# A two-layer float32 trunk: the last output group's weights in the rooms of two activation pairs, their norms put last, and the first chunks queued ahead of two weights

## The chip, the cores and the metric

One core of one Trainium2 chip runs the whole program. TensorE (PE) does the matmuls and transposes, VectorE (DVE) and ScalarE (ACT) the element work, GpSimd (POOL) some small work and the stores of hidden tiles and of the residual, SyncE (SP) issues all loads. The metric is the device time of one execution in microseconds (us). The kernel before took 2356.33 us, the median of three runs (2354.39 to 2356.82).

## The reference

Two layers over a sequence of 1024 tokens of width 1024, all float32. Layer 0 mixes tokens with a state-space model and a gated projection, layer 1 with a short gated convolution. Each is followed by a SwiGLU feed-forward part (FFN) and a gated per-layer embedding (PLE):

```python
for i in range(DEPTH):
    hn = rmsnorm(h, norm_mix_g[i])
    mix = s5_mixer(hn, ...) if i % 2 == 0 else shortconv_mixer(hn, ...)
    h = h + mix
    h = h + swiglu_ffn(rmsnorm(h, norm_ffn_g[i]), ffn_w_in[i], ffn_w_out[i])   # hidden width 2816
    gate = jax.nn.sigmoid(rmsnorm(h, norm_ple_g[i]) @ ple_w_gate[i])
    h = h + gate * (p[i] @ ple_w_up[i])
return rmsnorm(h, final_norm_g)
```

## The kernel before

A float32 matmul is done as three matmuls of reduced-precision parts (`mm3`, L121 to L124): each operand is split into a high part, rounded by an ACT cast (L87), and a low part, the rest, by a DVE subtract (L88); the products are high by high, high by low, low by high. Tokens stand in 8 tiles of 128, taken in the order 0, 4, 1, 5, 2, 6, 3, 7; tiles q and q+4 are pair q.

The FFN's hidden tensor (22 blocks of 128 columns) is written to DRAM (`hid`, by GpSimd, L322) and read back by `out_phase` (L326), which multiplies it with the output weights. It takes the 22 weights in three groups, of 8, 8 and 6. For a group it goes over the 8 tiles; a tile loads its hidden chunks (`ch`, four blocks each, L346; 512 KB for a full one), in the first group also the residual `h` (L348), runs 24 matmuls per full chunk (four weights, two halves of the columns, three products) into two PSUM banks (PE's shape in the rows: `psmm<-ulow,ch`, `psmm<-uhigh,ch` or `psmm<-w,ch`, by where the weight stands), and adds them to `h` (L360). The first group's weights are fetched ahead (L332). A weight of the next group marked early is fetched after a tile, one per tile (`soon`); the others when the group has ended (`late`). The same function serves `conv_out`, the output projection of the convolution, with 8 weights in two groups of 4.

Weights and activations share rooms in SBUF. `ulow[:, q]` is the room of pair q's activations or of two weights (`room_low(q, s)`); `uhigh` holds six weights (`room_high`); four more stand in `w8` tiles (`room_new`). In the FFN the groups stand in: the eight low rooms; high 0 to 5 and new 0, 1; new 2, 3 and high 0 to 3. The last four are late, since the second group's weights stand in high 0 to 3 until it ends.

Every load passes through one of four staging slots, `r0` to `r3` (`raw_tile`), taken in rotation in program order: weights before their split (`raw`, L100), chunks, and the normed tiles `xn` of `norm_pair` (L173). A tile gets its slot when the last reader of the tile four places earlier has ended, and SP issues its loads in order: what waits at its head holds all behind it.

After the last group each tile is handed on (`last_post`, L366). For the FFN that is `norm_tile`: the tile is normed, transposed and split into `ulow[:, q]`, from which the PLE part starts, tiles again in the order above. For `conv_out` it is `norm_pair` for the next FFN's first matrix, which uses a seven-product (Strassen-like) block scheme: pair q is normed when tile q+1 is handed on, pair 3 after tile 7. Of a pair, 4 blocks of transposes (L181) go to PE, 2 norms (`xn`, L173), 4 sums (L221 to L232) and 7 subtracts (L88) to DVE. The weights of the next matrix (`weights_set`, L268) need 4 sums (L275 to L283) and 7 subtracts on DVE.

The order of instructions on each engine comes from a scheduler that runs when the program is built. An engine executes its list in order.

Of the kernel before, what the change touches and what calls it, by code (L numbers as in the profile page):

```python
# [23 lines left out]
def trunk(  # L24
# [12 lines left out]
    KT = D // P  # L37
# [26 lines left out]
    HT = T // 2  # L64
# [17 lines left out]
    def psum(pool=None):  # L82
        pool = pool or mm
        return pool.tile([P, 512], F32, name="ps" + pool.name, tag="ps")
# [7 lines left out]
    def raw_tile(i=None, shape=(P, D), dt=F32, name="raw"):  # L92
        if i is None:
            slots.append(slots.pop(0))
        tag = slots[-1] if i is None else f"r{i}"
        return (uhp if tag == "r3" else rawp).tile(list(shape), dt, name=name, tag=tag)

    def load_raw(src, pattern, **kw):
        raw = raw_tile()
        nc.sync.dma_start(out=raw.rearrange(pattern, **kw), in_=src)  # L100
        return raw


    def slot_low(q, s):
        v = ulow[:, q, s * 2 * D:(s + 1) * 2 * D].rearrange("p (l n) -> p l n", l=2)
        return v[:, 0], v[:, 1]

    def slot_high(i):
        v = uhigh.rearrange("p c k l j -> p (c k l j)")[:, i * 2 * D:(i + 1) * 2 * D].rearrange("p (l n) -> p l n", l=2)
        return v[:, 0], v[:, 1]  # L110
# [5 lines left out]
    def unit_of(slot, raw):  # L116
        hi, lo = slot
        split(hi, lo, raw)
        return hi, lo

    def mm3(ps, ahi, alo, bhi, blo, start, stop, more=False):  # L121
        PE.matmul(ps, ahi, bhi, start=start, stop=False, skip_group_check=more)  # L122
        PE.matmul(ps, ahi, blo, start=False, stop=False, skip_group_check=more)  # L123
        PE.matmul(ps, alo, bhi, start=False, stop=stop, skip_group_check=more)  # L124
# [4 lines left out]
    def first():  # L129
        return tc.high_priority(offset=100)  # L130

    def square(t, cs):

        if "ms" not in squares:
            squares["ms"] = tiny.tile([P, T, 4], F32, name="ms", tag="ms")
        got = squares.setdefault(t, [])
        junk = t2_tile("junk", BF16, D)
        ms = squares["ms"][:, t, len(got):len(got) + 1]
        A.activation(junk[:, cs], h[t][:, cs], AF.Square, scale=1.0 / math.sqrt(D), accum_out=ms)  # L139
        got.append(ms)  # L140
# [13 lines left out]
    def load_gain(g_row):  # L154
        gb = tiny.tile([P, D], F32, name="gb", tag="gb")
        nc.gpsimd.dma_start(out=gb, in_=g_row.partition_broadcast(P))
        return gb
# [49 lines left out]
    def norm_pair(q, gb):  # L207
        t0, t1 = q, q + HT
        halves = 2 if q == HT - 1 else 1
        x0, x1 = normed(t0, gb, halves), normed(t1, gb, halves)  # L210

        def put(c, src):
            split(moving_part(c, 0, q), moving_part(c, 1, q), by_kt(src))

        p11, p12, p22 = transposed(x0, 0), transposed(x1, 0), transposed(x1, 1)
        p21 = transposed(x0, 1, mm)
        put(0, p11)
        b12 = t2_tile("b12")
        A.copy(b12, p12)
        T1 = t2_tile("T1")  # L220
        V.tensor_tensor(T1, b12, p11, ALU.subtract)  # L221
        T2 = t2_tile("T2")
        V.tensor_tensor(T2, p22, T1, ALU.subtract)
        put(1, T2)
        put(2, T1)
        put(3, p21)
        T3 = t2_tile("T3")
        V.tensor_tensor(T3, p22, b12, ALU.subtract)
        put(4, T3)
        put(5, p22)  # L230
        T4 = t2_tile("T4")
        V.tensor_tensor(T4, p21, T2, ALU.subtract)  # L232
        put(6, T4)

    def spill(t):
        nc.gpsimd.dma_start(out=hdram[t], in_=h[t])
# [89 lines left out]
    def out_phase(wout, groups, last_post, following=()):  # L326


        def fetch(ht, room):
            return unit_of(room(), load_raw(wout[ht], "p n -> p n"))  # L330

        units = {ht: fetch(ht, room) for ht, room, _ in groups[0]}  # L332
        for gi, group in enumerate(groups):
            last = gi == len(groups) - 1
            todo = [(early, lambda ht=ht, room=room: units.__setitem__(ht, fetch(ht, room)))
                    for ht, room, early in ([] if last else groups[gi + 1])]
            todo = todo or list(following)
            soon, late = [f for early, f in todo if early], [f for early, f in todo if not early]
            for t in ORDER:
                parts = {}  # L340
                for ht, *_ in group:
                    if ht // 4 not in parts:
                        parts[ht // 4] = ch = raw_tile(shape=(P, 4, 2, P), dt=F32R, name="ch")
                        of = [x[0] % 4 for x in group if x[0] // 4 == ht // 4]
                        ks = slice(min(of), max(of) + 1)
                        nc.sync.dma_start(out=ch[:, ks].bitcast(F32), in_=hid[ht // 4][t, :, ks])  # L346
                if gi == 0:
                    nc.sync.dma_start(out=h[t], in_=hdram[t])  # L348
                ps = [psum() for _ in range(2)]
                for j in parts:  # L350
                    mine = [x[0] for x in group if x[0] // 4 == j]
                    for nb in range(2):
                        cs = slice(nb * 512, (nb + 1) * 512)
                        for ht in mine:
                            ch = parts[j][:, ht % 4]
                            bhi, blo = (w[:, cs] for w in units[ht])
                            mm3(ps[nb], ch[:, 0], ch[:, 1], bhi, blo, ht == group[0][0], ht == group[-1][0])
                        if mine[-1] == group[-1][0]:
                            with first():
                                V.tensor_tensor(h[t][:, cs], ps[nb], h[t][:, cs], ALU.add)  # L360
                                if last:
                                    square(t, cs)
                if soon:
                    soon.pop(0)()
                if last:
                    last_post(t)  # L366
            for f in soon + late:
                f()

    def room_low(q, s):  # L370
        return lambda: slot_low(q, s)

    def room_high(i):
        return lambda: slot_high(i)

    def room_new(i):
        return lambda: slot_new(i)
# [18 lines left out]
    def ffn_out(l, post, following):  # L396
        rooms = [(room_low(q, s), False) for s in range(2) for q in range(HT)]
        rooms += [(room_high(i), True) for i in range(6)] + [(room_new(i), True) for i in range(4)]
        rooms += [(room_high(i), False) for i in range(4)]
        hts = [(ht, *room) for ht, room in enumerate(rooms)]  # L400
        cuts = [0, 8, 16, NHT]
        out_phase(ffn_w_out[l].rearrange("(ht p) n -> ht p n", p=P), [hts[a:b] for a, b in zip(cuts, cuts[1:])], post,
                  following)

    def ple_units(l, nb, rooms):

        wg = ple_w_gate[l].rearrange("(kt p) n -> p kt n", p=P)
        units = {}

        def fetch(u):  # L410
            raw = load_raw(wg[:, 2 * u:2 * u + 2, nb * 512:(nb + 1) * 512], "p (kt n) -> p kt n", kt=2)
            units[u] = [a.rearrange("p (kt n) -> p kt n", kt=2) for a in unit_of(rooms[u](), raw)]

        return units, [lambda u=u: fetch(u) for u in range(KT // 2)]
# [595 lines left out]
    def posted(gain, pairs):  # L1010

        gb = load_gain(gain)

        def pair(q):
            norm_pair(q, gb)
            spill(q)
            spill(q + HT)

        def post(t):
            if not pairs:  # L1020
                return norm_tile(t, gb)
            if 0 < t < HT:
                pair(t - 1)
            if t == T - 1:
                pair(HT - 1)
        return post
# [17 lines left out]
        h_tiles()  # L1044

    def ffn_ple(l, last):
        units, makers = ple_units(l, 0, [room_high(i) for i in (4, 5, 0, 1)])
        ffn_out(l, posted(norm_ple_g[l], False), [(i < 2, f) for i, f in enumerate(makers)])
        if last:
            gb = load_gain(final_norm_g)  # L1050
            ple(l, units, lambda t: final_tile(t, gb))
        else:
            ple(l, units, posted(norm_mix_g[l + 1], True))
# [12 lines left out]
    inner("f1", lambda: ffn_in(1), (11, 3, 7, 3))  # L1066
    outer("f1", 4)
    ffn_ple(1, True)
    release()

# [29 lines left out]
```

## Time and profile before

| | |
|---|---|
| median of 3 runs | 2356.33 us |
| profiled execution, time / span | 2359.43 us / 2357.5 us |
| PE busy, mean granted clock | 2247.0 us (95% of the span), 0.981 |
| DVE, ACT, POOL busy | 1331.9, 765.5, 163.1 us |

PE is busy nearly all the time, so what matters is where it stands still, what it waits for there, and where its granted clock is low. Layer 0's FFN output starts at 848 us and its last group at 1046 us of the span, layer 1's at 1998 and 2194 us; the convolution's output projection ends at 1557 us.

### The profile page before, as it was taken

How to read it: one execution, taken by the hardware profiler on the slowest of the kernel's cores; microseconds unless marked ns; L12 is line 12 of the kernel's file. 1: busy time of each engine (PE TensorE's matmuls, PEld its weight loads, DVE VectorE, ACT ScalarE, POOL GpSimd, SP SyncE). 2: the span in 40 equal slices, each digit the busy share in tenths (PEclk: the TensorE clock that was granted, in tenths of full speed). 3: DMA queues.
4: the chain of work that ended last, by engine and by line, in shares of the span. 5: the costliest groups of instructions: out<-in, count | busy, mean ns of one | idle time of the engine just before them, and what ended most of it. 6: DMA issues, size and time to landing. Idle time of an engine off the chain costs nothing.

```text
span 2357.5 us, 27090 instructions
## 1 busy us (share of the span) xinstructions
PE 2247.0 (95%) x10253; PEld 1835.7 (78%) x10253; DVE 1331.9 (56%) x2246; ACT 765.5 (32%) x1449; POOL 163.1 (7%) x268
## 2 busy tenths in 40 slices
PE   6888999899999999999979999989999999999998
PEld 4776887788888878878858888768888888788787
DVE  7785326866666642125488776487666666121454
ACT  6554223433333320013343332153333333000232
POOL 2110001000000000000000000010000001000000
PEclk8999999999999999999989999999999999999999
DMA  7555202333333364333232225434333335543333
GB/s 246 141 135 148 69 1 89 105 112 112 111 114 110 107 241 149 118 127 114 70 129 81 90 92 179 159 125 125 108 108 107 111 113 172 212 139 107 108 109 110
DMA packets 212978, 288.87 MB, mean 123 GB/s; under 512 B 21360, under 2 KB 152432, under 8 KB 212848
## 3 DMA queue, kind: packets, MB, share of 16 engines
q1 hardware_dynamic: 191520, 212.63, 29.0%
q0 software_dynamic: 20928, 74.47, 10.2%
q8 instruction: 80, 1.31, 0.2%
q14 instruction: 50, 0.41, 0.1%
q10 hardware_dynamic: 400, 0.04, 0.0%
HBM read 190.93 MB, written 79.69 MB: 115 GB/s over the span
## 4 chain that ended last, share of the span: by engine, by line
PE 85%; DMA 6%; DVE 5%; ACT 1%; SPq 1%; issue 1%; POOL 0%; DVEq 0%; POOLq 0%; ACTq 0%
PE psmm L122 27%; PE psmm L124 27%; PE psmm L123 27%; DMA ch<-hid 2%; PE pstr L181 1%; DMA raw<-in_ffn_w_out_dram 1%; DMA tw<-tmp 1%; DVE W L575 1%; DVE gv L925 1%; DMA h<-hd 1%; DVE tmp L575 1%; DVE ulow L88 1%; DVE uhigh L88 1%; PE pstr L874 0%; DVE raw L575 0%
## 5 line engine op out<-in xcount | busy, mean ns | idle before, releaser
L122 PE MATMUL psmm<-ulow,ws 128*128 128x512 f32 x896 | 351.1, 393 | 1.6 <-ACT s L301 1.6
L123 PE MATMUL psmm<-ulow,ws 128*128 128x512 f32 x896 | 350.6, 391 | 0.0
L124 PE MATMUL psmm<-ulow,ws 128*128 128x512 f32 x896 | 350.4, 391 | 0.0
L124 PE MATMUL psmm<-uhigh,ws 128*128 128x512 f32 x672 | 265.3, 395 | 0.0
L122 PE MATMUL psmm<-uhigh,ws 128*128 128x512 f32 x672 | 265.1, 394 | 0.0
L123 PE MATMUL psmm<-uhigh,ws 128*128 128x512 f32 x672 | 264.9, 394 | 0.0
L360 DVE TENSOR_TENSOR h<-psmm,h 128x512 f32<-128x512 f32 x128 | 88.0, 690 | 276.6 <-PE psmm L124 276.6
L88 DVE TENSOR_TENSOR ws<-raw,ws 128x512 fp32r<-128x512 f32 x224 | 153.6, 688 | 117.8 <-ACT ws L87 117.4
L87 ACT CAST ws<-raw 128x512 fp32r<-128x512 f32 x224 | 137.5, 619 | 213.0 <-PE psmm L124 211.2
L122 PEld LDWEIGHTS psmm<-ulow,ws 128*128 128x128 f32 x896 | 169.4, 189 | 39.5 <-ACT s L301 2.9
L123 PEld LDWEIGHTS psmm<-ulow,ws 128*128 128x128 f32 x896 | 169.4, 189 | 36.2
L124 PEld LDWEIGHTS psmm<-ulow,ws 128*128 128x128 f32 x896 | 169.2, 189 | 36.2
L87 ACT CAST ws<-st 128x512 fp32r<-128x512 f32 x168 | 104.0, 620 | 204.4 <-PE psmm L124 189.5
L123 PEld LDWEIGHTS psmm<-uhigh,ws 128*128 128x128 f32 x672 | 126.1, 188 | 30.3
L124 PEld LDWEIGHTS psmm<-uhigh,ws 128*128 128x128 f32 x672 | 126.1, 188 | 30.3
L122 PEld LDWEIGHTS psmm<-uhigh,ws 128*128 128x128 f32 x672 | 126.1, 188 | 29.1
L323 POOL DMA_DIRECT2D hid<-hs x104 | 78.2, 755 | 903.4 <-DVE hs L88 895.4
L122 PE MATMUL psmm<-ulow,ch 128*128 128x512 f32 x320 | 128.4, 401 | 10.8 <-DMA ch<-hid 10.8
L139 ACT ACTIVATE junk<-h 128x512 bf16<-128x512 f32 (+1 forms) x113 | 64.0, 567 | 204.0 <-DVE h L360 104.0
L87 ACT CAST uhigh<-raw 128x1024 fp32r<-128x1024 f32 x36 | 37.2, 1049 | 278.9 <-PE psmm L124 136.7
L123 PE MATMUL psmm<-ulow,ch 128*128 128x512 f32 x320 | 127.6, 399 | 0.0
L124 PE MATMUL psmm<-ulow,ch 128*128 128x512 f32 x320 | 127.5, 398 | 0.0
(240 smaller groups left out, 4238.5 us busy)
## 6 DMA issues: line engine op xcount, KB each, us to landing
hid<-hs POOLq DMA_DIRECT2D x104, 512.0 KB, 4.3
ch<-hid SPq DMA_DIRECT2D x96, 512.0 KB, 3.7
raw<-in_ffn_w_in_dram SPq DMA_DIRECT2D x88, 512.0 KB, 4.4
raw<-in_ffn_w_out_dram SPq DMA_DIRECT2D x44, 512.0 KB, 3.6
hd<-h POOLq DMA_DIRECT2D x24, 512.0 KB, 3.0
h<-hd SPq DMA_DIRECT2D x24, 512.0 KB, 8.7
raw<-in_conv_w_in_dram SPq DMA_DIRECT2D x24, 512.0 KB, 4.0
up<-ev SPq DMA_DIRECT2D x32, 256.0 KB, 3.2
```

Of the source, the lines that this page charges most:

```text
L87: A.copy(hi, src)
L88: V.tensor_tensor(lo, src, hi.bitcast(F32), ALU.subtract)
L122: PE.matmul(ps, ahi, bhi, start=start, stop=False, skip_group_check=more)
L123: PE.matmul(ps, ahi, blo, start=False, stop=False, skip_group_check=more)
L124: PE.matmul(ps, alo, bhi, start=False, stop=stop, skip_group_check=more)
L139: A.activation(junk[:, cs], h[t][:, cs], AF.Square, scale=1.0 / math.sqrt(D), accum_out=ms)
L181: PE.transpose(pt[:, c * P:(c + 1) * P], xn[:, kt * P:(kt + 1) * P], ident)
L323: nc.gpsimd.dma_start(out=hid[ht // 4][half * HT:(half + 1) * HT, :, ht % 4].rearrange("t p l j -> p t l j"), in_=hs.bitcast(F32))
L360: V.tensor_tensor(h[t][:, cs], ps[nb], h[t][:, cs], ALU.add)
L575: V.tensor_tensor(o, a, b, op)
L925: V.tensor_tensor_scan(gv[:, g, 1:P], dec, sv[:, g, 1:P], 0.0, ALU.mult, ALU.add)
```

## The change

It has four parts. The last group's weights 18 to 21 go into the low rooms of pairs 2 and 3, which hold weights of the first group and are free when that has ended; all are now early. The tiles 2, 6, 3 and 7 (`t % 4` of 2 and 3) are no longer handed on as they are finished but kept and handed on, in that order, after the last matmul, since pairs 2 and 3's rooms now hold weights until then; this stands in `out_phase` and so holds in `conv_out` too, where tile 2 hands on pair 1, tile 3 pair 2 and tile 7 pair 3. Of the first group only six weights are fetched ahead, and the other two behind the first tile's chunks and residual. The PLE part's first four gate weights go into high 0 to 3, all early.

```diff
-        units = {ht: fetch(ht, room) for ht, room, _ in groups[0]}
+        units = {ht: fetch(ht, room) for ht, room, _ in groups[0][:KT - 2]}
+        kept = []
...
                 if gi == 0:
                     nc.sync.dma_start(out=h[t], in_=hdram[t])
+                for ht, room, _ in groups[0]:
+                    if ht not in units:
+                        units[ht] = fetch(ht, room)
...
                 if soon:
                     soon.pop(0)()
-                if last:
+                if last and t % HT < HT // 2:
                     last_post(t)
+                elif last:
+                    kept.append(t)
             for f in soon + late:
                 f()
+        for t in kept:
+            last_post(t)
...
         rooms += [(room_high(i), True) for i in range(6)] + [(room_new(i), True) for i in range(4)]
-        rooms += [(room_high(i), False) for i in range(4)]
+        rooms += [(room_low(q, s), True) for q in (2, 3) for s in range(2)]
...
     def ffn_ple(l, last):
-        units, makers = ple_units(l, 0, [room_high(i) for i in (4, 5, 0, 1)])
-        ffn_out(l, posted(norm_ple_g[l], False), [(i < 2, f) for i, f in enumerate(makers)])
+        units, makers = ple_units(l, 0, [room_high(i) for i in range(4)])
+        ffn_out(l, posted(norm_ple_g[l], False), [(True, f) for f in makers])
```

SP at the start of layer 0's FFN output, before (`hid_99` and `hid_100` are the first two chunks of each tile, `hd` the residual):

```order
L100 DMA raw<-in_ffn_w_out_dram 128x1024 x8
L346 DMA ch<-hid_99 128x1024
L346 DMA ch<-hid_100 128x1024
L100 DMA raw<-in_ffn_w_out_dram 128x1024
L348 DMA h<-hd 128x1024 x2
L346 DMA ch<-hid_99 128x1024
L348 DMA h<-hd 128x1024 x6
L346 DMA ch<-hid_100 128x1024
```

The same of the change:

```order
L100 DMA raw<-in_ffn_w_out_dram 128x1024 x6
L347 DMA ch<-hid_99 128x1024
L347 DMA ch<-hid_100 128x1024
L100 DMA raw<-in_ffn_w_out_dram 128x1024 x2
L347 DMA ch<-hid_100 128x1024
L349 DMA h<-hd 128x1024 x3
L100 DMA raw<-in_ffn_w_out_dram 128x1024
L349 DMA h<-hd 128x1024 x2
L100 DMA raw<-in_ffn_w_out_dram 128x1024
L349 DMA h<-hd 128x1024 x3
L347 DMA ch<-hid_99 128x1024 x3
```

The first tile's two chunks move from behind eight weights to behind six. The second tile's (tile 4's) first chunk, `hid_99`, moves from the 12th place to the 20th, behind all eight residual loads; its second chunk, `hid_100`, moves ahead of them. On PE tile 4 still begins with `hid_99`.

PE at the end of the convolution's output projection, before (`xn` are normed tiles of pairs 2 and 3, `pstr` and `psmm` PSUM banks, `psmm_11676` the first product of the next FFN):

```order
L124 MATMUL psmm_11538<-w8_10993,ch_11535 128x512
L181 MATMUL pstr_11494<-ident_72,xn_11487 128x128 x4
L181 MATMUL pstr_11499<-ident_72,xn_11487 128x128 x4
L181 MATMUL psmm_11598<-ident_72,xn_11573 128x128 x4
L181 MATMUL pstr_11583<-ident_72,xn_11573 128x128 x4
L181 MATMUL pstr_11588<-ident_72,xn_11580 128x128 x4
L181 MATMUL pstr_11593<-ident_72,xn_11580 128x128 x4
L122 MATMUL psmm_11676<-ulow_81,ws_11649 128x512
```

The same of the change:

```order
L124 MATMUL psmm_11422<-w8_10993,ch_11419 128x512
L181 MATMUL pstr_11465<-ident_72,xn_11457 128x128 x4
L181 MATMUL pstr_11470<-ident_72,xn_11463 128x128 x4
L181 MATMUL pstr_11475<-ident_72,xn_11463 128x128 x4
L181 MATMUL psmm_11480<-ident_72,xn_11457 128x128 x4
L181 MATMUL psmm_11538<-ident_72,xn_11515 128x128 x4
L181 MATMUL pstr_11523<-ident_72,xn_11515 128x128 x4
L181 MATMUL psmm_11598<-ident_72,xn_11573 128x128 x4
L181 MATMUL pstr_11528<-ident_72,xn_11521 128x128 x4
L181 MATMUL pstr_11533<-ident_72,xn_11521 128x128 x4
L181 MATMUL pstr_11583<-ident_72,xn_11573 128x128 x4
L181 MATMUL pstr_11588<-ident_72,xn_11580 128x128 x4
```

Behind the last matmul stand 12 blocks of transposes (the twelfth, `pstr_11593`, behind the first ffn matmul) where there were 6. Six blocks that stood between the output matmuls have gone behind them.

DVE in the same place, of the change: a stretch that ends with the split of the fourth weight operand of the next FFN, which its 15th matmul before (its 13th in the change) reads (`raw_11645`, `raw_11647` are its first two loads, `raw_11785`, `raw_11787` the second two; `T` and `b12` a pair's sums):

```order
L278 TENSOR_TENSOR st_11655<-raw_11647,raw_11645 128x512
L275 TENSOR_TENSOR st_11792<-raw_11785,raw_11787 128x512
L223 TENSOR_TENSOR T2_11609<-pstr_11593,T1_11607 128x512
L228 TENSOR_TENSOR T3_11617<-pstr_11593,b12_11605 128x512
L88 TENSOR_TENSOR ulow_81<-T1_11607,ulow_81 128x4x128
L276 TENSOR_TENSOR raw_11787<-raw_11787 128x512
L88 TENSOR_TENSOR ws_11657<-st_11655,ws_11657 128x512
L88 TENSOR_TENSOR ws_11660<-raw_11647,ws_11660 128x512
L232 TENSOR_TENSOR T4_11623<-psmm_11598,T2_11609 128x512
L88 TENSOR_TENSOR ws_11663<-raw_11645,ws_11663 128x512
```

The sum `st_11792`, which reads the fourth load, stands here ahead of pair 3's second sum and of `ws_11663`; before it stood behind both. From the last add to `h` to `ws_11663` DVE has before 22 instructions of 128 x 512 (L88, L221 to L232, L275 to L283) and two half norms; in the change 38, one whole norm and four half norms.

## Rows read from the trace of the kernel before

**Rows 1.** The page, part 1: busy time, share of span, instructions.

```profile
PE 2247.0 (95%) x10253; PEld 1835.7 (78%) x10253; DVE 1331.9 (56%) x2246; ACT 765.5 (32%) x1449; POOL 163.1 (7%) x268
```

**Rows 2.** Timeline of PE, both layers' last group: start, length, what, [idle before, releaser].

```profile
1040.22 0.50 PE L123 MATMUL psmm<-uhigh,ch 128*128 128x512 f32 x1 [0.53 <-DVE uhigh L88]
...
1045.66 0.80 PE L122 MATMUL psmm<-w,ch 128*128 128x512 f32 x1 [4.24 <-DMA ch<-hid]
...
2188.66 0.50 PE L123 MATMUL psmm<-uhigh,ch 128*128 128x512 f32 x1 [0.45 <-DVE uhigh L88]
...
2194.22 0.79 PE L122 MATMUL psmm<-w,ch 128*128 128x512 f32 x1 [4.35 <-DMA ch<-hid]
```

**Rows 3.** Windows behind those stalls: busy per engine, then clock, DMA share, GB/s.

```profile
1045.66:1053.66 8.00, 8.00 (x23) 6.29 (x23) 1.23 (x1) 1.05 (x1) 0.00 (x0) 0.62 0.15 49
...
2194.22:2202.22 8.00, 8.00 (x26) 6.40 (x27) 1.23 (x1) 1.05 (x1) 0.00 (x0) 0.72 0.14 43
```

**Rows 4.** Timeline of PE, second tile of the FFN output, both layers.

```profile
869.58 0.80 PE L122 MATMUL psmm<-ulow,ch 128*128 128x512 f32 x1 [4.59 <-DMA ch<-hid]
...
2018.07 0.80 PE L122 MATMUL psmm<-ulow,ch 128*128 128x512 f32 x1 [3.45 <-DMA ch<-hid]
```

**Rows 5.** Windows of the FFN output's first two tiles.

```profile
848.00:859.20 11.20, 11.20 (x49) 9.14 (x49) 6.05 (x8) 2.31 (x4) 1.50 (x2) 1.00 0.98 347
859.20:869.58 10.38, 5.79 (x25) 4.33 (x24) 0.69 (x1) 0.00 (x0) 0.56 (x1) 0.90 1.03 416
869.58:877.58 8.00, 8.00 (x25) 6.42 (x26) 1.82 (x2) 1.04 (x1) 0.00 (x0) 0.71 0.23 92
...
2008.85:2018.07 9.22, 5.77 (x26) 4.32 (x24) 0.69 (x1) 0.00 (x0) 0.56 (x1) 0.98 1.03 415
```

**Rows 6.** Timeline of SP at that start: issue, length, what (the last row is layer 1's).

```profile
846.47 0.33 SPq L100 DMA_DIRECT2D raw<-in_ffn_w_out_dram  x1
...
849.34 3.57 SPq L348 DMA_DIRECT2D h<-hd  x6
853.94 1.59 SPq L346 DMA_DIRECT2D ch<-hid  x2
...
2004.19 1.58 SPq L346 DMA_DIRECT2D ch<-hid  x2
```

**Rows 7.** DMA issues from 840 to 867 us: count, size, median us to landing.

```profile
h<-hd SPq DMA_DIRECT2D x8, 512.0 KB, 10.7
ch<-hid SPq DMA_DIRECT2D x6, 512.0 KB, 7.2
```

**Rows 8.** Timeline of PE behind the convolution's last output matmul.

```profile
1556.98 1.04 PE L181 MATMUL pstr<-ident,xn 128*128 128x128 f32 x8
1557.86 0.60 PE L181 MATMUL psmm<-ident,xn 128*128 128x128 f32 x4
...
1569.69 1.97 PE L181 MATMUL pstr<-ident,xn 128*128 128x128 f32 x8 [10.71 <-DVE xn L173]
...
1576.24 0.50 PE L122 MATMUL psmm<-ulow,ws 128*128 128x512 f32 x1 [0.22 <-ACT s L301]
```

**Rows 9.** Windows before and behind it.

```profile
1514.00:1557.00 43.00, 43.00 (x208) 35.29 (x207) 33.28 (x59) 18.80 (x44) 8.20 (x14) 1.00 0.40 147
...
1558.90:1569.70 10.80, 0.09 (x2) 0.01 (x1) 8.41 (x17) 5.09 (x12) 0.86 (x1) 0.73 0.60 187
```

**Rows 10.** Groups on DVE, 1514 to 1569.7 us: busy us, mean ns, idle before.

```profile
L173 DVE SCALAR_TENSOR_TENSOR xn<-h,rs,gb 128x1024 f32<-128x1024 f32 x6 | 7.7, 1279 | 2.1 <-POOL rs L148 2.1
L88 DVE TENSOR_TENSOR uhigh<-T,uhigh 128x512 fp32r<-128x512 f32 x6 | 4.1, 680 | 0.0
...
L173 DVE SCALAR_TENSOR_TENSOR xn<-h,rs,gb 128x512 f32<-128x512 f32 x4 | 2.8, 750 | 0.6 <-POOL rs L148 0.6
...
L275 DVE TENSOR_TENSOR st<-raw 128x512 f32<-128x512 f32 x1 | 0.7, 693 | 1.8 <-DMA raw<-in_ffn_w_in_dram 1.8
```

**Rows 11.** DMA issues, 1557 to 1580 us.

```profile
raw<-in_ffn_w_in_dram SPq DMA_DIRECT2D x5, 512.0 KB, 4.4
```

## The prediction

> **What bounds the kernel now.** I read the busy shares first, then PE's timeline for its idle times, then the windows around each for clock and DMA share, then the SP queue and the DMA landings. PE is busy in 2247.0 of the span's 2357.5 us [rows 1], so a change that leaves the number of matmuls as it is can win or lose only where PE stands still, or runs slowly behind such a place. The edits touch three kinds of place.
>
> At the border of the second and last output group PE waits twice in each layer: 0.53 us for the subtract of a late weight and 4.24 us for a hidden chunk in layer 0, 0.45 and 4.35 us in layer 1 [rows 2]. The reader is to see the two releasers: first the last of four weights, then the chunk whose staging slot these weights held. In the 8 us behind, the granted clock is 0.62 and 0.72 of full and only 23 and 26 matmuls run [rows 3].
>
> At the start of the FFN output the second tile (tile 4) waits 4.59 and 3.45 us for its second chunk [rows 4]. In these 20 us the DMA engines are full: share 0.98, then 1.03, at 347 and 416 GB/s [rows 5]. So the place in the queue decides when a chunk lands: the chunk issued at 853.94 [rows 6] is used at 869.58, 15.6 us later, although the median for a chunk here is 7.2 and for a residual load 10.7 us [rows 7].
>
> At the end of the convolution's output projection PE has 16 transposes left, then stands 10.71 us for a normed tile, and gets to the 15th matmul of the next FFN at 1576.24 [rows 8]. Before the last matmul DVE is busy for 33.28 of 43.00 us, beside a PE that never stops; in the idle stretch it is busy for 8.41 of 10.80 us [rows 9]. So DVE bounds this stretch, and what it does ahead of the last matmul is free.
>
> **Border of the last two groups.** All six weights are now fetched one per tile beside 48 matmuls, and no slot is left waiting for a late weight; the chunk of the next tile is then issued behind a weight that was split long before. I take both stalls as gone: 0.53 + 4.24 + 0.45 + 4.35 = 9.6 us. With them goes the slow clock behind: 8 x (1 - 0.62) = 3.0 and 8 x (1 - 0.72) = 2.2 us. Together **-14.8**. Bounds: 0, if another load of the same stretch is late instead, and -14.8; I take the full amount, since four of the six weights leave the border and DVE and ACT are nearly idle there (1.23 and 1.05 of 8 us).
>
> **Start of the FFN output.** The first tile's chunks move ahead of two weights, but the first tile was not waiting: PE runs through from 848.00 to 859.20 [rows 5], and it still has its work until 859.2. The second tile's first chunk pays. By the rotation of slots it takes the one of the first tile's second chunk, which is read until the first tile ends, 859.2 (before it took that of a weight fetched ahead). It also stands behind all eight residual loads and two more weights in SP's queue, where before it was the 12th of that stretch. From the first weight on, 22 transfers of 512 KB lie up to and including it; before, 21 up to the one waited for. GpSimd's stores run beside both. The engines are full, so one more transfer at 416 GB/s is 0.524 MB / 416 = 1.26 us: it lands at 869.54 + 1.26 = 870.8. At 869.58 PE had, before, 24 of the second tile's matmuls behind it, which took 869.58 - 4.59 - 859.20 = 5.79 us; in the change none. Loss 1.3 + 5.8 = 7.05 us. In layer 1 the same: 2018.07 - 3.45 - 2008.85 = 5.77, plus 1.26, 7.03. Together **+14.1**, as stalls of 11.6 and 10.4 us where 4.59 and 3.45 stood. The slow clock behind (0.71 [rows 5]) is there in both.
> Bounds: the chunk, issued at 859.2, can land as soon as 4.4 us later, which is a load's median where little else runs [rows 11]: 863.6, which gives 863.6 - 869.6 + 5.8 = -0.2, in layer 1 2013.25 - 2018.07 + 5.77 = +1.0, together +0.8. Or it takes as long as the chunk before did, 15.6 us (in layer 1, issued 2004.19 [rows 6], 13.8): +11.0 and +10.4, together +21.4. I take +14.1, by the bytes, because the share is full on both sides of 859.2.
> Here the rows show that a load issued last into full engines landed last, 15.6 us against a median of 7.2 [rows 6, 7]. The Trainium skill, "DMA: Bandwidth & Descriptors", section "Queues, rings and completion order", says that on each DMA engine the descriptors of one issuing engine are consumed in ring order; by that rule putting a load later in SP's queue makes it land later by all that is ahead, which speaks against this edit and gives the +14.1; were the loads served side by side instead, it would be near the lower bound.
>
> **End of the convolution's output.** `conv_out` shares the loop, so tiles 2 and 3 hand on pairs 1 and 2 only behind the last matmul. Nothing there needed it: its rooms are not the FFN's. PE: 6 blocks of four transposes leave the matmuls, at (1557.86 - 1556.98) / 2 = 0.44 us [rows 8], so the last matmul ends 2.6 us earlier. DVE, from the last add to the fourth weight operand: 38 instead of 22 instructions at 0.68 us, 10.9 more; one whole norm at 1.28 and two half norms at 0.75 more, 2.8 [rows 10]. 13.7 together. And `st_11792`, which reads the fourth load of the next FFN, now stands ahead of pair 3's sums and of that operand: the slot of that load is that of pair 3's second normed tile, free only when its last transposes have run, so DVE stands for a load, 4.4 us [rows 11]; before it came behind. Behind DVE wait the operands, and so PE. Sum -2.6 + 13.7 + 4.4 = **+15.5**.
> Bounds: without the wait, and with DVE's idle 10.80 - 8.41 = 2.4 us of before filled up, 13.7 - 2.6 - 2.4 = +8.7. With the load before it uncovered as well (the one that `st_11652` reads), 15.5 + 4.4 = +19.9. I take the middle value: the order shows the one wait plainly, and of the other 1.8 us were waited for before, too [rows 10].
>
> **Edits at nothing.** In the FFN the tiles 2, 6, 3, 7 are normed behind the last matmul. The PLE part begins with 0, 4, 1, 5, each 24 matmuls, some 4 x 24 x 0.23 = 22 us of PE, and four norms of one 1.28 and two 0.68 us subtracts are 10.6 us of DVE [rows 10]: hidden. Without that cover it is up to 10.6 us a layer. The PLE's gate weights in rooms free since the second group come earlier and cost nothing.
>
> **Sum.** -14.8 + 14.1 + 15.5 = +14.8 us on the profiled 2359.43 us: 2374.2. The median of the runs is 3.1 us below the profiled execution, so from 2356.33: **2371.1 us**.
>
> **Rivals.**
> 1. The queue is dry when the chunk comes (not slower): by 859.2 most of the loads ahead have landed, and the chunk takes 4.4 us. It decides from a landing before 864 us. -14.8 + 0.8 + 15.5 = +1.4, 2357.8 us. For it: the median chunk lands in 7.2 us, half of the 15.6 [rows 7]. Against: 416 GB/s until 869.58 [rows 5].
> 2. The convolution's end is cheap: DVE fills its gaps and the load is there in time, +8.7. Sum +8.0, 2364.3 us. For it: DVE idles 2.4 of 10.8 us. Against: the in-order place of `st_11792`.
> 3. Both: -14.8 + 0.8 + 8.7 = -5.3, 2351.0 us, faster.
> 4. The change doesn't do what it says at the border: a chunk is late there still, and the 14.8 us stay. 14.1 + 15.5 = +29.6, 2385.9 us. For it: the stall's larger part is a chunk, not a weight [rows 2]. Against: the chunk's slot was held by the late weights.
>
> **How the numbers follow.** A difference below 0.2%, 4.7 us, can't be told from none. Forecast 0.58, rival 1 0.14, rival 2 0.11, rival 3 0.10, rival 4 0.07. Faster: rival 3, 0.10. Same: rival 1, 0.14. Slower: 0.58 + 0.11 + 0.07 = 0.76. The range runs from 2355 (just under rival 1, leaving out rival 3) to 2386 (rival 4; also the upper bounds of both losses, -14.8 + 21.4 + 19.9 = +26.5, 2382.8).
>
> **What would show it.** No idle of PE over 1 us where the last group starts, and a clock of 1.0 there. One wait of 10 to 12 us for a chunk at the end of the first tile, in both layers, with that chunk issued no earlier than the first tile's end. Behind the convolution's last matmul some 35 us to the 15th FFN matmul where 19.3 stood, with DVE idle for a load. The prediction is wrong if the chunk lands within 5 us of its issue, or if that last stretch grows by less than 8 us.

## The result and the profile after

The changed kernel takes 2368.26 us (median of 5 runs, 2366.18 to 2368.90) against 2356.82 us of the kernel before in the same session: ratio 1.0044, 95% interval 1.0031 to 1.0057. It is slower by 11.4 us; 2371.1 was forecast, a loss of 14.8. The profiled span grows by 9.0 us, from 2357.5 to 2366.5. One execution of all that were timed, of the version with the doubled DVE work in the loop, took 5319.01 us and is left out of its median.

PE's timeline of the changed kernel: the two long waits at the start of the FFN output, layer 0 and layer 1 (start, length, what, idle before and its releaser), to set beside [rows 4].

```profile
871.28 0.79 PE L122 MATMUL psmm<-ulow,ch 128*128 128x512 f32 x1 [13.46 <-DMA ch<-hid]
...
2027.97 0.80 PE L122 MATMUL psmm<-ulow,ch 128*128 128x512 f32 x1 [12.66 <-DMA ch<-hid]
```

The same chunk in SP's timeline, layer 0: what is issued ahead of it, and when.

```profile
837.04 2.06 SPq L347 DMA_DIRECT2D ch<-hid  x2
841.20 2.10 SPq L100 DMA_DIRECT2D raw<-in_ffn_w_out_dram  x2
847.99 0.33 SPq L347 DMA_DIRECT2D ch<-hid  x1
848.36 1.37 SPq L349 DMA_DIRECT2D h<-hd  x3
849.85 0.77 SPq L100 DMA_DIRECT2D raw<-in_ffn_w_out_dram  x1
850.72 0.99 SPq L349 DMA_DIRECT2D h<-hd  x2
852.26 0.33 SPq L100 DMA_DIRECT2D raw<-in_ffn_w_out_dram  x1
852.64 2.19 SPq L349 DMA_DIRECT2D h<-hd  x3
857.85 21.45 SPq L347 DMA_DIRECT2D ch<-hid  x4
```

The chunk is issued at 857.85, when the first tile ends, behind eight residual loads and two weights, and lands 13.4 us later. (Counted from the first weight, it has gone from the 14th place in SP's order to the 22nd, not from the 12th to the 20th.) The queue also stands still from 843.3 to 847.99, for the staging slot of tile 4's other chunk, which the seventh weight holds until it has landed and DVE has split it. SP's waits from 843.3 to 848 us (who waited for what: total, times, longest), and the windows of 845 to 849 us:

```profile
SPq L347 <- DVE ulow L88: 2.3, 1, 2.3
SPq L347 <- DMA raw<-in_ffn_w_out_dram: 2.2, 1, 2.2
...
845.00:847.00 2.00, 2.00 (x11) 1.60 (x10) 0.96 (x2) 1.40 (x3) 0.00 (x0) 1.00 0.53 209
847.00:849.00 2.00, 2.00 (x10) 1.65 (x9) 1.95 (x2) 0.97 (x1) 0.00 (x0) 1.00 0.05 12
```

The DMA share falls to 0.05: the DMA engines have next to nothing to move. The windows of the first tile, of the wait and behind it (busy time per engine, clock, DMA share, GB/s) answer [rows 5]; the last two rows are layer 1's first tile, in the changed kernel and before.

```profile
846.60:857.82 11.22, 11.22 (x49) 8.76 (x47) 5.82 (x7) 2.29 (x4) 1.49 (x2) 1.00 0.76 263
857.82:871.28 13.46, 0.00 (x0) 0.00 (x0) 3.14 (x3) 2.09 (x2) 0.56 (x1) 0.64 1.03 416
871.28:879.28 8.00, 8.00 (x27) 6.38 (x28) 0.00 (x0) 0.00 (x0) 0.00 (x0) 0.75 0.12 47
...
2004.10:2015.31 11.21, 11.20 (x49) 8.75 (x47) 5.39 (x7) 2.24 (x4) 1.51 (x2) 1.00 0.81 272
...
1997.60:2008.85 11.25, 11.25 (x49) 9.02 (x49) 4.85 (x7) 2.19 (x3) 1.51 (x2) 1.00 0.98 375
```

The first tile moves 263 GB/s where it moved 347, in layer 1 272 where it moved 375: that is what the queue's standstill costs, and it is paid behind the tile.

At the border of the last two groups (windows of the changed kernel, layer 0, against [rows 2, 3]) PE has no idle time and its clock stays full, and so it is in layer 1 from 2188 to 2228 us:

```profile
1030.00:1050.00 20.00, 20.00 (x88) 16.27 (x87) 4.12 (x7) 2.50 (x5) 0.52 (x1) 1.00 0.33 110
1050.00:1070.00 20.00, 20.00 (x96) 16.37 (x96) 11.78 (x17) 7.16 (x15) 1.12 (x3) 1.00 0.44 144
```

Behind the convolution's last matmul one wait of 10.71 us [rows 8] has become five, 12.8 us together:

```profile
1554.61 0.40 PE L124 MATMUL psmm<-w,ch 128*128 128x512 f32 x1
...
1558.98 0.66 PE L181 MATMUL psmm<-ident,xn 128*128 128x128 f32 x4 [1.10 <-DVE xn L173]
...
1565.52 1.12 PE L181 MATMUL pstr<-ident,xn 128*128 128x128 f32 x4 [5.28 <-ACT b L219]
1568.09 1.97 PE L181 MATMUL pstr<-ident,xn 128*128 128x128 f32 x8 [1.46 <-DVE uhigh L88]
1572.11 1.12 PE L181 MATMUL pstr<-ident,xn 128*128 128x128 f32 x4 [1.44 <-ACT b L219]
1580.19 0.50 PE L122 MATMUL psmm<-ulow,ws 128*128 128x512 f32 x1 [3.54 <-ACT s L301]
```

The windows of the 40 us from the last output matmul on show what sets the pace (two of 20 us each, of the changed kernel and then of the one before):

```profile
1554.60:1574.60 20.00, 10.70 (x55) 8.28 (x54) 19.23 (x32) 11.65 (x22) 1.50 (x2) 0.67 0.34 107
1574.60:1594.60 20.00, 16.43 (x63) 12.62 (x63) 20.00 (x34) 13.40 (x23) 0.00 (x0) 0.90 0.33 97
...
1557.00:1577.00 20.00, 9.06 (x42) 7.38 (x41) 16.99 (x30) 12.19 (x25) 1.44 (x2) 0.74 0.43 132
1577.00:1597.00 20.00, 20.00 (x89) 16.35 (x88) 18.54 (x32) 10.18 (x18) 0.00 (x0) 1.00 0.36 106
```

DVE (third busy figure) works 39.23 of 40.00 us, where it worked 35.53; of the releasers named, ACT waits for DVE's results itself (5.1 us for the sums of L221 alone). In these 40 us PE's timeline has 105 products of the next FFN before and 67 here.

The span by stages, from the timelines of both (us):

| stage | before | after | change |
|---|---|---|---|
| start to first matrix of FFN 0 | 420.58 | 418.90 | -1.7 |
| FFN 0, first matrix, to the second output group | 523.75 | 532.40 | +8.7 |
| second and last output group, layer 0 | 168.26 | 159.11 | -9.2 |
| PLE 0 and convolution's first matrix | 341.76 | 343.66 | +1.9 |
| convolution's output to FFN 1's end of first output tile | 554.50 | 561.24 | +6.7 |
| from there to the second output group | 83.23 | 93.17 | +9.9 |
| second and last output group, layer 1 | 168.26 | 159.10 | -9.2 |
| PLE 1 and the end | 97.16 | 98.92 | +1.8 |

The +1.9 and the +1.8 are transposes of the kept tiles, 16 in each layer, which have moved from the last group into the PLE part; so the border's net gain is 2 x 9.2 - 1.9 - 1.8 = 14.7 us. The -1.7 in the first stage, where the program is unchanged, shows how far two executions differ.

### The profile page after: what moved, and what is told of

Read it like the earlier page. It is cut to its first block, busy times and chain, and to the rows that moved or that the text cites. A ratio compares the mean times of both kernels' runs of the same rounds, so it can differ in the third digit from the quotient of the medians.

```text
span 2366.5 us, 27093 instructions
## 1 busy us (share of the span) xinstructions
PE 2250.9 (95%) x10253; PEld 1839.2 (78%) x10253; DVE 1333.2 (56%) x2246; ACT 767.7 (32%) x1449; POOL 161.2 (7%) x268
## 4 chain that ended last, share of the span: by engine, by line
PE 87%; DVE 3%; DMA 2%; ACT 1%; issue 0%; POOL 0%; DVEq 0%; POOLq 0%; ACTq 0%
PE psmm L122 28%; PE psmm L124 28%; PE psmm L123 28%; DMA ch<-hid 1%; PE pstr L181 1%; DVE ulow L88 0%; PE pstr L948 0%; PE pstr L950 0%; PE pstr L949 0%; DVE xn L173 0%; PE pstr L882 0%; DVE uhigh L88 0%; DMA W<-W 0%; DVE W L583 0%; DVE gv L933 0%
## 5 line engine op out<-in xcount | busy, mean ns | idle before, releaser
L88 DVE TENSOR_TENSOR ws<-raw,ws 128x512 fp32r<-128x512 f32 x224 | 153.5, 687 | 117.1 <-ACT ws L87 117.0
L122 PE MATMUL psmm<-ulow,ch 128*128 128x512 f32 x448 | 179.3, 401 | 28.4 <-DMA ch<-hid 28.4
L123 PE MATMUL psmm<-ulow,ch 128*128 128x512 f32 x448 | 179.1, 400 | 0.0
L124 PE MATMUL psmm<-ulow,ch 128*128 128x512 f32 x448 | 178.9, 399 | 0.0
L122 PEld LDWEIGHTS psmm<-ulow,ch 128*128 128x128 f32 x448 | 85.7, 191 | 50.0 <-DMA ch<-hid 27.0
```

Source lines behind the costliest of these rows:

```text
L88: V.tensor_tensor(lo, src, hi.bitcast(F32), ALU.subtract)
```

## The experiments

Theory: three independent parts, border -14.7, start of the FFN output +18.6, end of the convolution +6.7. Each median below stands beside runs of the kernel before on the same chip (medians of 2355.7 to 2357.6).

**The convolution hands its tiles on in the loop.**

```diff
-                if last and t % HT < HT // 2:
+                if last and (t % HT < HT // 2 or not following):
```

> The changed kernel, but the convolution's output projection hands its tiles on inside the loop again (kept only in the FFN). Theory: the three parts of the change add up, and the convolution's part costs 6.7 us (DVE saturated for 40 us behind the last matmul): 2368.3 - 6.7 = 2361.6 us; the wait before the 15th FFN matmul falls from 3.5 back to some 0.2 us, the 10.7 us wait for a normed tile comes back. Rival: the slow start of the second FFN has another cause than the kept pairs: 2368 us, no change.

2363.60 us, ratio 1.0032 (1.0021 to 1.0044): 4.7 us below the changed kernel's median, 6.6 us by the spans (2359.9). PE's waits from 1550 to 1600 us (who waited for what: total, times, longest):

```profile
PE pstr L181 <- DVE xn L173: 11.5, 1, 11.5
PE psmm L122 <- ACT ws L87: 1.6, 1, 1.6
```

The single long wait is back, as expected; the 3.5 us one has become one of 1.6, where some 0.2 was expected. The pairs put last cost time. By the medians it is less than the 6.7 expected, and this pair of runs alone is at the 4.7 us that the prediction couldn't tell from none; a second pair follows below.

**All eight weights ahead again.**

```diff
-        units = {ht: fetch(ht, room) for ht, room, _ in groups[0][:KT - 2]}
+        units = {ht: fetch(ht, room) for ht, room, _ in groups[0]}
```

> The changed kernel, but all eight weights of the first group are fetched ahead of the first chunks again. Theory: the 13.5 and 12.7 us waits at the end of the first tile come from this edit alone, by the place it gives the second tile's first chunk: they fall back to about 4.6 and 3.5 us in the middle of the second tile, 2368.3 - 18.3 = 2350.0 us. Rival: the waits come from the loads of the last group's new rooms or from the longer list of early weights: waits of 12 us stay, 2368 us.

2347.18 us, ratio 0.9965 (0.9953 to 0.9978): 21.1 us below the changed kernel, 16.5 by the spans (the profiled execution, 2353.12 us, is the slowest of the five). PE's timeline, layers 0 and 1:

```profile
868.25 0.79 PE L122 MATMUL psmm<-ulow,ch 128*128 128x512 f32 x1 [3.96 <-DMA ch<-hid]
...
2017.91 0.80 PE L122 MATMUL psmm<-ulow,ch 128*128 128x512 f32 x1 [4.33 <-DMA ch<-hid]
```

The waits are the old ones again, though the new rooms and the longer list of early weights are kept. The rival falls: "first chunks ahead" makes the start slow.

**Only the new rooms:** both edits above.

> Only the new rooms, with the kept norms in the FFN alone and all eight weights fetched ahead. Theory: the border's 14.8 us and nothing else, 2356.8 - 14.8 = 2342.0 us, no wait of PE at the border of the last two groups. Rival: the parts don't add up, since the earlier weights of the last group need the first chunks' edit or load the start: 2350 us or more, with a wait left at the border or a longer one at the start.

2342.99 us, ratio 0.9941 (0.9927 to 0.9955): 13.4 us faster than before, against 14.8. PE waits at the border in neither layer. The parts add up: taking the first-chunk edit away from the version with the convolution in the loop gives 2363.60 - 2342.99 = 20.6, from the changed kernel 21.1; putting the convolution back gives 4.7 and 2347.18 - 2342.99 = 4.2. In this second pair every run of the one is slower than every run of the other.

**Residual loads held back.** With the first chunks ahead as in the change, each residual load from the third tile on waits for the first chunk of the tile before:

```diff
-            for t in ORDER:
+            for n, t in enumerate(ORDER):
+                if gi == 0 and n > 1:
+                    V.tensor_copy(h[t][:, 0:1], parts[0][:, 0, 0, 0:1].bitcast(F32))
+                    nc.sync.dma_start(out=h[t], in_=hdram[t])
...
-                if gi == 0:
+                if gi == 0 and n < 2:
                     nc.sync.dma_start(out=h[t], in_=hdram[t])
```

> The changed kernel, but the residual loads of the tiles from the third on are each issued only when the first chunk of the tile before has landed (a one-column copy ahead of each load makes it wait), so they don't stand ahead of the second tile's first chunk. Theory: that chunk's slot still comes free only at the end of the first tile, but with empty queues it lands some 4 to 5 us after its issue: waits of about 5 us in place of 13.5 and 12.7, 2368.3 - 16 = 2352 us. Rival: the slot and the weights make the wait, the residual loads don't matter: waits of 11 us or more, 2365 us or more.

2348.20 us, ratio 0.9964 (0.9952 to 0.9976): 20.1 us below the changed kernel. PE's timeline and SP's issue of the chunk, layer 0:

```profile
860.11 0.79 PE L122 MATMUL psmm<-ulow,ch 128*128 128x512 f32 x1 [5.87 <-DMA ch<-hid]
```

```profile
854.26 3.61 SPq L350 DMA_DIRECT2D ch<-hid  x3
```

The chunk is still issued only when the first tile has ended, but lands 5.8 us later in place of 13.4. In layer 1 the wait is 5.10 us. So some 7.6 us of each wait were the residual loads ahead in the queue (six are held back; six transfers of 1.26 us, by 416 GB/s, are 7.6), and what is left begins with the slot. The rest of the 20.1 us isn't all at this place: `out_phase` serves the convolution too, and its output projection, from first to last product, takes 97.6 us where it took 100.5.

**One weight behind the chunks instead of two**, in the version just shown, so that the rotation gives tile 4's first chunk another slot:

```diff
-        units = {ht: fetch(ht, room) for ht, room, _ in groups[0][:KT - 2]}
+        units = {ht: fetch(ht, room) for ht, room, _ in groups[0][:KT - 1]}
```

> The version of the changed kernel with the gated residual loads (six weights ahead; 2348.2 us, waits of 5.9 and 5.1 us), with seven weights ahead instead of six. Theory: what is left of the wait is the staging slot's: with six ahead the rotation gives the second tile's first chunk the slot that is read until the first tile ends; with seven it gets the slot of the first tile's first chunk, free half a tile, 5.6 us, earlier. The waits of 5.9 and 5.1 us fall to 1 us or less, and the slow clock behind (some 3 us each) goes with them: 2348.2 - 11 to 16 = 2332 to 2337 us. Rival: it is the landing time and the two weights queued near it, whichever slot: waits of 3 us or more stay, 2344 us or more.

2334.42 us, ratio 0.9908 (0.9891 to 0.9924): 13.8 us less. SP's timeline and PE's wait:

```profile
848.50 5.61 SPq L350 DMA_DIRECT2D ch<-hid  x3
```

```profile
855.50 0.50 PE L122 MATMUL psmm<-ulow,ch 128*128 128x512 f32 x1 [1.42 <-DMA ch<-hid]
```

The chunk's issue moves from the end of the first tile to its middle, and 5.87 us become 1.42 (in layer 1 5.10 become 0.44). From issue to landing the chunk takes 7.0 us, no less than the 5.85 of the version above, so it is the earlier issue that shortens the wait. The slot made the rest of it.

**DVE work doubled behind the convolution.** In the changed kernel, for pairs 1 and 2, each low part is written twice:

```diff
         def put(c, src):
-            split(moving_part(c, 0, q), moving_part(c, 1, q), by_kt(src))
+            hi, lo = moving_part(c, 0, q), moving_part(c, 1, q)
+            split(hi, lo, by_kt(src))
+            if q in twice:
+                V.tensor_tensor(lo, by_kt(src), hi.bitcast(F32), ALU.subtract)
...
     def conv_out(post):
+        twice.extend((1, 2))
```

> The changed kernel, in which for pairs 1 and 2 of the convolution's output each of the seven low parts is written twice by DVE (the same value, 14 subtracts more; 11 of them stand ahead of the fourth weight operand in DVE's order). Theory: behind the last matmul DVE is the bound, at 0.60 us a step: 11 x 0.60 = 6.6, at most 14 x 0.60 = 8.4 us longer, 2368.3 + 7 = 2375 us. Rival: the loads of the next FFN or PE's transposes set that stretch: 2 us or less, 2369 us.

2373.80 us, ratio 1.0077 (1.0063 to 1.0091): 5.5 us above the changed kernel, 5.0 by the spans. Its windows from the last matmul on:

```profile
1553.00:1573.00 20.00, 6.18 (x41) 4.73 (x40) 19.56 (x33) 7.67 (x15) 1.50 (x2) 0.66 0.25 79
1573.00:1593.00 20.00, 14.66 (x55) 10.81 (x54) 20.00 (x35) 11.06 (x20) 0.00 (x0) 0.82 0.33 96
```

DVE is full as before, and PE's timeline has 44 products of the next FFN where the changed kernel has 67: the work added to DVE comes out in the time, somewhat under the 6.6 that 11 subtracts were to cost and far from the rival's 2. DVE bounds the stretch.

**The same with the pairs in the loop:**

> The same 14 subtracts in the version with the new rooms only, where pairs 1 and 2 are handed on inside the loop, pair 1 well ahead of the last matmul. Theory: what DVE does beside the output matmuls is free; only what pair 2 has left behind the last matmul counts, at most 7 x 0.60 = 4.2 us: 2343.0 + 0 to 4, 2345 us. Rival: DVE bounds there too (it is busy for 33 of 43 us): 2343.0 + 7, 2350 us.

2347.44 us, the median of four executions, ratio 0.9961 (0.9947 to 0.9975): 4.45 us above the version with the rooms only, 3.6 by the spans. That lies between the two answers, just above the theory's 0 to 4. Seven of the 14 added subtracts start ahead of the last matmul and seven behind it. In the 40 us ahead of it DVE is busy for 33.36 us, against 32.01 without the doubling: 1.35 us more, where seven subtracts of 0.60 make 4.2, so other work of DVE has moved behind. The claim that DVE work ahead of the last matmul is free is not shown by it: what is added there can push something else behind.

**The best version:** only the new rooms, and the residual loads held back.

> Only the new rooms (kept norms in the FFN alone, eight weights ahead), and the residual loads from the third tile on issued after the first chunk of the tile before. Theory: the start's waits (3.6 and 2.8 us in the version with the rooms only, and a granted clock below 1 behind them) come from residual loads ahead of the second tile's second chunk; its slot is free in the middle of the first tile and with empty queues it lands before it is needed: no wait of PE at the start, 2343.0 - 6.4 and some 3 to 4 us of slow clock, 2333 us. Rival: the waits are the slot's, the residual loads only hide them: waits of 3 us stay, 2342 us.

2327.69 us, ratio 0.9878 (0.9863 to 0.9893): 1.2% faster than the kernel before. The windows of the FFN output's start, layer 0:

```profile
840.00:860.00 20.00, 20.00 (x87) 16.12 (x86) 10.91 (x15) 5.45 (x7) 2.05 (x3) 1.00 0.97 356
860.00:880.00 20.00, 20.00 (x87) 16.08 (x87) 5.39 (x8) 2.09 (x2) 0.00 (x0) 1.00 0.71 238
```

PE has no wait there in either layer. The gain on the version with the rooms only is 15.3 us, where 10 was expected. By the timelines the FFN's stretch from the first product of its output to the second group is 6.7 us shorter in layer 0 and 4.3 in layer 1: waits of 3.61 and 2.77 us and the slow clock behind them. The other 3.7 us are in the convolution's output projection, which holds its residual loads back by the same edit and which the expectation left out.

## Why the prediction was right, and which of its terms were not

**Border, -14.8.** Right in mechanism and size: -14.7 in the profile, -13.4 by the version with the rooms only. Both waits are gone in both layers, with the slow clock behind them. Rival 4 is out.

**Start, +14.1.** Right in mechanism, too small in size: the waits are 13.46 and 12.66 us instead of 11.6 and 10.4, and undoing the edit gives 21.1 or 20.6 us by the medians, 16.5 or 17.5 by the spans. The upper bound, +21.4, holds them. The step that failed is "the share is full on both sides of 859.2". It was full before; in the change the share in the first tile is 0.76 and 0.81, since the queue waits for a slot, and the loads not moved there, (347 - 263) x 11.2 / 524 = 1.8 transfers in layer 0 and (375 - 272) x 11.2 / 524 = 2.2 in layer 1, are moved in front of the chunk. At 1.26 us each that is 5.1 us, near the 4.5 that the stage table has above the forecast, 18.6 against 14.1. I had counted what stands ahead in the queue, but not that the queue's order, changed, would itself stand still. That a load lands by what is ahead of it, as [rows 6, 7] had it, is shown by the held-back residual loads: 13.4 us from issue to landing became 5.8. The Trainium skill, "DMA: Bandwidth & Descriptors", section "Queues, rings and completion order", says that on each DMA engine the descriptors of one issuing engine are consumed in ring order. The two landing times agree with it. Rival 1, a landing within 5 us of the issue, is out, and rival 3 with it.

**End of the convolution, +15.5.** The side was right, the size was not: 6.7 us in the stage table, 4.2 to 4.7 by the medians, below the lower bound of 8.7. The traces agree on it: from the last output matmul to the end of FFN 1's first output tile it is 460.7 to 461.5 us in four with the pairs put last (the changed kernel, eight weights ahead, the two with six or seven ahead and residual loads held back), 452.1 to 454.0 in three with the pairs in the loop (before, the convolution in the loop, only the new rooms); from the first output matmul to the last, the changed kernel and the one with eight ahead need 1.9 to 3.7 us less than those three. Three steps of the sum failed. DVE's timeline has the last add to `h`, the sums that read loads, and the fourth weight operand, before:

```profile
1557.18 0.69 DVE L360 TENSOR_TENSOR h<-psmm,h 128x512 f32<-128x512 f32 x1 [0.39 <-PE psmm L124]
...
1565.26 0.69 DVE L275 TENSOR_TENSOR st<-raw 128x512 f32<-128x512 f32 x1 [1.83 <-DMA raw<-in_ffn_w_in_dram]
...
1575.12 0.68 DVE L88 TENSOR_TENSOR ws<-raw,ws 128x512 fp32r<-128x512 f32 x1
```

and in the changed kernel:

```profile
1555.05 0.69 DVE L364 TENSOR_TENSOR h<-psmm,h 128x512 f32<-128x512 f32 x1 [1.12 <-PE psmm L124]
...
1570.75 0.69 DVE L275 TENSOR_TENSOR st<-raw 128x512 f32<-128x512 f32 x1 [0.32 <-DMA raw<-in_ffn_w_in_dram]
...
1577.36 0.68 DVE L275 TENSOR_TENSOR st<-raw 128x512 f32<-128x512 f32 x1
1577.97 0.68 DVE L223 TENSOR_TENSOR T<-pstr,T 128x512 f32<-128x512 f32 x1
...
1582.18 0.67 DVE L88 TENSOR_TENSOR ws<-raw,ws 128x512 fp32r<-128x512 f32 x1
```

First, "DVE stands for a load, 4.4 us" failed: DVE reaches `st_11792` at 1577.36 with no idle time, since its backlog lasts at least as long as the load. Second, the added work fills time in which DVE stood before: the first sum, waited for 1.83 us before, is waited for 0.32, and in the whole stretch the listed waits shrink from 2.7 to 0.3 us. Third, the instructions were priced by their busy 0.68 us, but one starts 0.60 us behind the other (0.61 from 1577.36 to 1577.97), so the 13.7 us of work are some 12. From the last add to the operand it is 27.1 us; before, 1575.12 - 1557.18 = 17.9. That is 9.2 us more, where 13.7 + 4.4 = 18.1 were counted; less the 2.1 us by which the last matmul ends earlier, 7.1, near the 6.7 of the stage table. The Trainium skill, "VectorE: DVE Perf Modes", section "The DRAIN you can't avoid", says that after an instruction the pipeline is flushed, and that a next one that isn't held starts earlier than the end of that flush. The trace agrees as far as starts 0.60 us apart beside 0.68 us of busy time go; whether these instructions are held doesn't show in it.

Rival 2's condition for this term, DVE filling its gaps and the load there in time, is what happened, and its +8.7 is too dear only by the third step.

**The sum** came out near by luck as much as by reasoning: the errors had opposite signs, start some 5 too small, convolution some 9 too large. Of the forecast's signs to look for, the missing waits at the border and the chunk issued no earlier than the first tile's end came true. The third did not, neither DVE idle for a load nor 35 us to the 15th FFN matmul. The matmul that was the 15th starts 25.3 us behind the last output matmul (1554.85 to 1580.19), 6.1 more than the 19.3 before. The prediction had called itself wrong for less than 8 us more in that stretch, and for this part it was.

## What to carry to other kernels

"Queue it first" helps only a load that is waited for, and in an in-order queue with rotating slots it shifts every later load to another slot: write down for each which reader's end frees its slot, and where the queue will stand still. Loads without a reader in the next microseconds (the residual, here) are worth holding back until the urgent ones have landed; on top of the new rooms that gave 15 us. When an edit sits in a helper, look at each of its callers: the convolution paid for a rule that only the FFN needed, and gained 3.7 of those 15 us from one that was written for the FFN.

## What the runs showed of the hardware

The slow clock behind a wait hardly depended on the wait's length: in the 8 us behind waits of 4.24, 4.35 and 4.59 us the mean granted clock was 0.62, 0.72 and 0.71 [rows 3, 5], behind 13.46 us 0.75. With several waits, the last of 3.54 us ending at 1580.19, it was 0.67 and then 0.90 in the two stretches of 20 us behind the convolution, against 0.74 and 1.00 before, where one wait of 10.71 us ends at 1569.69.

A load that waits for its slot at the head of SP's queue leaves the DMA engines without work: the share fell from 1.03 (843 to 845 us) to 0.05 (847 to 849 us).
